# Up projections of a gated ConvFFN: from feature-major, one feature tile at a time, to token-major, four at a time

## The chip, the core and the metric

The kernel runs on one core of a Trainium2 chip. The metric is the device time in microseconds, as the median of several runs. A core has TensorE (PE, matrix products; its weight loads are listed as PEld), VectorE (DVE), ScalarE (ACT), GpSimd (POOL) and SyncE (SP), each with a queue of its own that is worked off in order; SP and POOL issue the DMAs here.

## The reference

The model is an encoder of two layers over 256 tokens with 2048 channels. The even layer has a dilated-window and a differential attention, the odd one a grouped-query and a neighbourhood attention; each layer ends in a gated ConvFFN. Only the ConvFFN and what lies next to it are changed:

```python
D_MODEL = 2048; SEQ = 256; DEPTH = 2; D_FF = 5632; CONV_W = 3

def conv_ffn(x, w_up, conv_w, conv_b, w_down):
    h = jnp.einsum("bsd,df->bsf", x, w_up)
    g, u = h[..., :D_FF], h[..., D_FF:]
    gp = jnp.pad(g, ((0, 0), (1, 1), (0, 0)))
    g = conv_w[0] * gp[:, :-2] + conv_w[1] * gp[:, 1:-1] + conv_w[2] * gp[:, 2:] + conv_b
    return jnp.einsum("bsf,fd->bsd", jax.nn.gelu(g) * u, w_down)

def reference(...):
    for layer in range(DEPTH):
        ...
        h = h + mix.astype(h.dtype)
        f = conv_ffn(rmsnorm(h, ln_ffn[layer]), ...)
        h = h + f.astype(h.dtype)
    return rmsnorm(h, ln_final)
```

All inputs are float32. The gate g and the factor u have 5632 features each, which are 44 tiles of 128. The convolution runs along the tokens.

## The kernel before

**Numbers.** Every operand of a product is split into a high part of type fp32r and the rest, also fp32r; a product is the sum high x high, low x high and high x low. `split` (L239) does it: ScalarE casts the high part (L240), VectorE subtracts it (L243). Weights come in units of 128 x 1024 values (512 KB): `wunit` (L116) loads one on SP's queue into one of RAW = 5 buffers and splits it into one of four pairs wh, wl.

**Two forms of a product.** In the feature-major form, `gemm_b` (L151), the weight block of 128 x 128 is stationary and the activations move: `b_high` (L140, matmul at L142) streams 512 columns, the 256 tokens of the high and of the low part side by side; `b_low` (L146, matmul at L148) streams the 256 tokens of the high part once more for wl. The result has features on the partitions and two halves of 256 columns, which `halves` (L230) adds: ScalarE copies one (L233), VectorE adds the other (L234) and multiplies by the row factor of the RMS norm (L236), which has to be broadcast over the partitions for it (`row_broadcast`, L337, two TensorE transposes). In the token-major form, `gemm_a` (L208), 128 tokens of the activations are stationary and 512 features of the weights move (`a_products`, L198, matmuls at L204 to L206): for each unit two blocks of 128 channels, two token halves and three products, twelve matmuls. The result has tokens on the partitions, in two PSUM banks.

**The ConvFFN** (`ffn`, L789). The 44 feature tiles are worked in two halves of 22, since the product tiles of more than 24 don't fit. For each tile one `gemm_b` gives gate and factor, VectorE convolves along the tokens (three instructions, L810, L812, L814), ScalarE applies GELU (L816), VectorE multiplies (L818) and the product is split into a tile prod. After 22 tiles the down projection runs token-major over four chunks of 512 channels (`finish_chunk(gemm_a(...))`), each of 11 units, and VectorE adds its result to the residual h (L361).

**From residual to the next product.** After the last half, the squares of each chunk are summed on ScalarE (L274). Chunks 0 to 2 are turned to feature-major by `turned_rows` (L317): VectorE transposes 32 x 32 blocks within a 128 x 1024 tile (L320), and `moved` (L278) puts the blocks in place by 16 DMAs of 32 KB, by turns from POOL's and SP's queue (L282). Then ScalarE and VectorE make the split tiles yT. Chunk 3 is turned by TensorE (`transposes`, L309, at L305). `mixer_out` (L369) does the output projection of the attention in the same way, but works chunks 0 and 1 side by side up to the last unit, so that the last attention head has time to arrive. The attention uses the pair `turned` (L286) and `moved` for its probabilities.

**The order of the work.** The program is written out flat. `later(delay, fn)` (L91) keeps a step for a later tick; `tick` (L95) is called after every second unit of a `gemm_a` and twice in a `gemm_b`, and emits what is due; `flush` (L103) emits all that is pending. When the program is built, the framework plans the order of each engine's queue from the order of emission and from durations that it assumes; buffers that are not yet free hold an instruction back. What is marked `keep_in_program_order` stays where it was emitted. On the chip each queue then runs in that fixed order, and an instruction that waits holds back those behind it.

**The end.** `finish_all` (L1010) does the last down projection, chunk by chunk, with the final norm; the last four units of chunk 3 are split ahead and worked first for one half of the tokens, then for the other.

## Time and profile before

| | us |
|---|---|
| median of 3 runs | 2456.17 (2455.28 to 2456.97) |
| profiled execution | 2455.45 |
| its span, first to last instruction | 2453.7 |
| TensorE busy | 2441.5 (100%) |
| VectorE busy | 1631.3 (66%) |
| ScalarE busy | 1261.4 (51%) |
| GpSimd busy | 165.2 (7%) |

The page of the profile lists busy times, the chain of work that ended last (followed back from the last instruction), and the costliest groups of instructions with the idle time ahead of them and what ended it. The views of the trace used here are: the chain in order of time (start, length, what), TensorE's waits (us in all, times, longest), a timeline by engine (start, length, instruction, and in brackets the idle time before it and its releaser), and tables of busy time by stretch. A mean in ns is that of one instruction from its start to its end; matmuls overlap, so the distance of their starts is shorter than that.

### The profile page before, as it was taken

To read this page: it belongs to the slowest core of one execution; us is meant where nothing else is said; L and a number is where in the kernel's file an instruction comes from. 1 tells how busy PE (TensorE), PEld (TensorE's weight loads), DVE (VectorE), ACT (ScalarE), POOL (GpSimd) and SP (SyncE) were. 2 spreads that over 40 slices of the span, in tenths; PEclk is the share of its full clock that TensorE was granted. 3 is DMA by queue.
4 is the path that set the end of the run, shared out by engine and by line. 5 is a ranking of instruction groups with operands and counts; after the bars stand their busy time and mean duration, and the time that the engine had idled before them with its cause. 6 is when DMAs were issued, how large, how long until landed. Compare 5 with 4: busy or idle time off the path is not lost.

```text
span 2453.7 us, 35020 instructions
## 1 busy us (share of the span) xinstructions
PE 2441.5 (100%) x12958; PEld 2110.6 (86%) x12958; DVE 1631.3 (66%) x2472; ACT 1261.4 (51%) x1876; POOL 165.2 (7%) x292
## 2 busy tenths in 40 slices
PE   9999999999999999999999999999999999999998
PEld 8888888888888888888888888888888888888887
DVE  6577577677677774476775567766777754676754
ACT  6455455565654543445444557545555533545443
POOL 1011012011200000000001100332000000000000
PEclk9999999999999999999999999999999999999999
DMA  8566566555655566555556655657556565555564
GB/s 309 183 201 194 171 190 207 177 183 196 208 173 199 180 198 202 182 193 185 195 193 202 218 186 157 192 170 243 180 182 197 183 208 191 180 194 185 197 197 146
DMA packets 183212, 474.00 MB, mean 193 GB/s; under 512 B 65144, under 2 KB 66936, under 8 KB 183040
## 3 DMA queue, kind: packets, MB, share of 16 engines
q1 hardware_dynamic: 173264, 460.03, 56.9%
q0 software_dynamic: 9344, 11.08, 2.5%
q8 instruction: 101, 1.65, 0.3%
q10 hardware_dynamic: 432, 0.66, 0.1%
q14 instruction: 71, 0.58, 0.1%
HBM read 458.48 MB, written 2.18 MB: 188 GB/s over the span
## 4 chain that ended last, share of the span: by engine, by line
PE 97%; DVE 1%; issue 1%; ACT 0%; DMA 0%; POOL 0%; SPq 0%; DVEq 0%; ACTq 0%
PE gm L142 38%; PE gm L148 20%; PE gm L205 12%; PE gm L204 12%; PE gm L206 12%; PE tp L305 0%; DMA room<-scc 0%; POOL room L282 0%; PE s L426 0%; PE s L428 0%; PE s L427 0%; PE s L661 0%; DVE wl L243 0%; SPq L282 0%; PE s L622 0%
## 5 line engine op out<-in xcount | busy, mean ns | idle before, releaser
L243 DVE TENSOR_TENSOR wl<-raw,wh 128x1024 fp32r<-128x1024 f32 (+1 forms) x860 | 1034.3, 1216 | 558.2 <-ACT wh L240 325.7
L240 ACT CAST wh<-raw 128x1024 fp32r<-128x1024 f32 (+1 forms) x860 | 897.2, 1047 | 704.5 <-PE gm L206 377.6
L142 PE MATMUL gm<-yT,wh 128*128 128x512 f32 x4096 | 954.6, 390 | 0.0
L142 PEld LDWEIGHTS gm<-yT,wh 128*128 128x128 f32 x4096 | 760.6, 188 | 153.9 <-DVE yT L249 1.0
L148 PEld LDWEIGHTS gm<-yT,wl 128*128 128x128 f32 x4096 | 507.6, 192 | 9.2
L148 PE MATMUL gm<-yT,wl 128*128 128x256 f32 x4096 | 511.9, 283 | 0.0
L204 PE MATMUL gm<-wh,prod 128*128 128x512 f32 x702 | 273.1, 389 | 0.0
L205 PE MATMUL gm<-wl,prod 128*128 128x512 f32 x702 | 273.1, 389 | 0.0
L206 PE MATMUL gm<-wh,prod 128*128 128x512 f32 x702 | 273.1, 389 | 0.0
L233 ACT COPY t<-gm 128x256 f32<-128x256 f32 x256 | 95.4, 373 | 283.1 <-PE gm L148 282.9
L204 PE MATMUL gm<-wh,yT 128*128 128x512 f32 x412 | 161.2, 392 | 0.0
L205 PE MATMUL gm<-wl,yT 128*128 128x512 f32 x412 | 160.8, 390 | 0.0
L206 PE MATMUL gm<-wh,yT 128*128 128x512 f32 x412 | 160.7, 390 | 0.0
L205 PEld LDWEIGHTS gm<-wl,prod 128*128 128x128 f32 x702 | 131.8, 188 | 27.4
L204 PEld LDWEIGHTS gm<-wh,prod 128*128 128x128 f32 x702 | 131.8, 188 | 27.4
L206 PEld LDWEIGHTS gm<-wh,prod 128*128 128x128 f32 x702 | 131.8, 188 | 27.1
L234 DVE TENSOR_TENSOR t<-t,gm 128x256 f32<-128x256 f32 x256 | 105.6, 413 | 1.5 <-ACT t L233 1.3
L205 PE MATMUL gm<-wl,mix 128*128 128x512 f32 x256 | 100.0, 390 | 2.1 <-DVE wl L243 2.1
L204 PE MATMUL gm<-wh,mix 128*128 128x512 f32 x256 | 100.0, 390 | 0.6 <-ACT mix L246 0.6
L206 PE MATMUL gm<-wh,mix 128*128 128x512 f32 x256 | 99.3, 389 | 0.0
L282 POOL DMA_DIRECT2D hT<-z x72 | 41.5, 584 | 780.9 <-ACT junk L274 681.0
L206 PEld LDWEIGHTS gm<-wh,yT 128*128 128x128 f32 x412 | 77.4, 188 | 16.1
(248 smaller groups left out, 1640.0 us busy)
## 6 DMA issues: line engine op xcount, KB each, us to landing
raw<-in_up SPq DMA_DIRECT2D x352, 512.0 KB, 4.3
raw<-in_down SPq DMA_DIRECT2D x176, 512.0 KB, 4.3
raw<-in_eva_qk SPq DMA_DIRECT2D x96, 512.0 KB, 4.2
raw<-in_eva_v SPq DMA_DIRECT2D x46, 512.0 KB, 4.4
raw<-in_evb_qk SPq DMA_DIRECT2D x32, 512.0 KB, 4.1
raw<-in_ev_out SPq DMA_DIRECT2D x32, 512.0 KB, 4.6
raw<-in_od_qk SPq DMA_DIRECT2D x32, 512.0 KB, 4.4
raw<-in_od_out SPq DMA_DIRECT2D x32, 512.0 KB, 4.4
```

The lines of the kernel that those rows point to most:

```text
L142: T.matmul(ps.rearrange("p a b -> p (a b)"), wh[:, k * P:(k + 1) * P], act[u * 8 + k].rearrange("p a b -> p (a b)"), start=(u == 0 and k = ...
L148: T.matmul(ps[:, 1, :], wl[:, k * P:(k + 1) * P], act[u * 8 + k][:, 0, :], start=False, stop=(last and u * 8 + k == KT - 1))
L204: T.matmul(ps[t], ah, wh[:, sl], start=(kt == 0), stop=False)
L205: T.matmul(ps[t], ah, wl[:, sl], start=False, stop=False)
L206: T.matmul(ps[t], al, wh[:, sl], start=False, stop=(kt == nk - 1))
L233: S.copy(t0, ps[:, 0, :])
L234: V.tensor_tensor(t0, t0, ps[:, 1, :], op=ALU.add)
L240: first = S.copy(dst_h, src)
L243: V.tensor_tensor(dst_l, src, dst_h.bitcast(F32), op=ALU.subtract)
L282: (nc.sync if i % 2 else G).dma_start(dst[j * 32:(j + 1) * 32, :, i * 32:(i + 1) * 32], z[i * 32:(i + 1) * 32].rearrange("p (b j c) -> p b ...
```

## The change

The up projections use `gemm_a`: a group is four feature tiles, and each of its two sides (gate, factor) is one product of 8 units with 512 features. ScalarE scales the result by the row factor on its way out of PSUM, VectorE transposes the 32 x 32 blocks, and 16 DMAs move them into a feature-major tile of 128 x 1024 (a quad). Two ticks later the four gate tiles are convolved, and GELU is applied to all four at once; two ticks after the factor's product the four are multiplied and split. The halves have 24 and 20 tiles, that is 6 and 5 groups. The down projection works its first two chunks side by side up to the last two units of each, which need the last group's tiles. The attention's q and k tiles lie in quads of the same size as the pairs of before; the differential attention's turned probabilities and the xT tiles of the start lie in other buffers. The weights of up and down are laid out in the new order of units on the host.

```diff
@@ -288,9 +288,6 @@
         V.transpose(p, p)
         moved(p, dst)
 
-    def new_turned(tag, n=4, pool=att):
-        return pool.tile([P, n, P], F32, name=nm("pf"), tag=tag, bufs=1)
-
     def y_tile(src, gain, kt, pin=False):
         y = acts.tile([P, 2, SEQ], F32R, name=nm("yT"), tag="yT", bufs=KT)
         dst = [y[:, x, :] for x in range(2)]
@@ -395,8 +392,13 @@
             return pairs[slot - slot % 2][:, slot % 2]
         return acts.tile([P, 2, SEQ], F32R, name=nm(name), tag=f"act{slot}")
 
+    def quad(slot, dtype=F32):
+        return att.tile([P, 4, SEQ], dtype, name=nm("qk"), tag=f"qk{slot}", bufs=1)
+
     def new_qk(name, slot):
-        return att.tile([P, 2, SEQ], F32R, name=nm(name), tag=f"qk{slot}", bufs=1)
+        if slot % 2 == 0:
+            pairs["qk", slot] = quad(slot, F32R)
+        return pairs["qk", slot - slot % 2][:, slot % 2 * 2:slot % 2 * 2 + 2, :]
 
     def qk_sum(ps, r, order, slot):
         t = halves(ps, r, order)
@@ -488,12 +490,12 @@
 
 
     def x_load(u):
-        t = att.tile([P, 2, SEQ], F32, name=nm("xT"), tag=f"qk{2 + u % 4}", bufs=1)
+        t = acts.tile([P, 2, SEQ], F32, name=nm("xT"), tag=f"act{u % 4}")
         nc.sync.dma_start(t.rearrange("p a b -> p (a b)"), a["xT"][u])
         return t
 
     ln = load("ln", (P, 4, KT), eng=nc.sync)
-    xt0 = att.tile([P, 2, SEQ], F32, name=nm("xT"), tag="qk2", bufs=1)
+    xt0 = acts.tile([P, 2, SEQ], F32, name=nm("xT"), tag="act0")
     nc.scalar.dma_start(xt0[:, 0, :], a["xT"][0, :, 0:SEQ])
     zeros = tmp.tile([P, SEQ], F32R, name="zeros", tag="rx")
     V.memset(zeros.bitcast(F32), 0.0)
@@ -737,7 +739,7 @@
             V.tensor_scalar(w[:, t, 1, :], w[:, t, 1, :], den[:, t, 1:2], None, op0=ALU.mult)
             V.scalar_tensor_tensor(w[:, t, 0, :], w[:, t, 0, :], den[:, t, 0:1], w[:, t, 1, :],
                                    op0=ALU.mult, op1=ALU.add)
-        pf = new_turned(f"qk{4 + hd % 2}")
+        pf = b_room[:, hd % 2 * 4:hd % 2 * 4 + 4]
         turned(sc[0][:, 0, :], pf)
         later(3, lambda: b_transposes(hd, pf, vt), 1)
 
@@ -774,6 +776,7 @@
             split_scaled(natural(y[:, 0, :]), natural(y[:, 1, :]), parity_rev(ps[:, f, :]), sub_gain[:, f:f + 1])
             mix[8 + 2 * hd + f] = y
 
+    b_room = quad(4).rearrange("p a (b c) -> p (a b) c", c=P)
     for pair in range(2):
         vt = v_tiles(gemm_a(a["evb_v"][pair], yT, KT), rstd_par, range(20 - 4 * pair, 24 - 4 * pair))
         for hd in (2 * pair, 2 * pair + 1):
@@ -786,46 +789,76 @@
     yT = mixer_out(a["ev_out"], mix, ln[:, 2, :])
 
 
+    def up_group(layer, j, yT, rstd, prod):
+
+        sides = {}
+        for x in range(2):
+            ps = gemm_a(a["up"][layer, j, x], yT, KT, hooks={6: flush} if not (j or x) else {})
+            if not (j or x):
+                rstd.append(row_factor())
+            z = new_sc().rearrange("p t (f k) -> p (t f) k", k=P)
+            for t in range(2):
+                S.activation(z.rearrange("p (f t) k -> p t f k", t=2)[:, t], ps[t].rearrange("p (f k) -> p f k", k=P),
+                             AF.Copy, scale=rstd[0][:, t:t + 1])
+            sides[x] = quad(2 * x)
+            turned(z.rearrange("p b k -> p (b k)"), sides[x].rearrange("p f (t k) -> p (f t) k", k=P))
+            if not x:
+                later(2, lambda: convolved(layer, j, sides))
+        later(2, lambda: multiplied(j, sides, prod))
+
+    def convolved(layer, j, sides):
+
+        g4, c4 = sides[0], quad(4)
+        sides[2] = c4
+        for i in range(4):
+            f = 4 * j + i
+            g, c = g4[:, i, :], c4[:, i, :]
+            V.tensor_scalar(c, g, convw[:, layer, 1, f:f + 1], convb[:, layer, f:f + 1], op0=ALU.mult, op1=ALU.add)
+            V.scalar_tensor_tensor(c[:, 1:SEQ], g[:, 0:SEQ - 1], convw[:, layer, 0, f:f + 1],
+                                   c[:, 1:SEQ], op0=ALU.mult, op1=ALU.add)
+            V.scalar_tensor_tensor(c[:, 0:SEQ - 1], g[:, 1:SEQ], convw[:, layer, 2, f:f + 1],
+                                   c[:, 0:SEQ - 1], op0=ALU.mult, op1=ALU.add)
+        S.activation(c4, c4, AF.Gelu_apprx_tanh)
+
+    def multiplied(j, sides, prod):
+
+        u4, c4 = sides[1], sides[2]
+        V.tensor_tensor(c4, c4, u4, op=ALU.mult)
+        for i in range(4):
+            y = new_act("prod", (4 * j + i) % NACT)
+            split(y[:, 0, :], y[:, 1, :], c4[:, i, :])
+            prod.append(y)
+
+    def first_two(src, act, nk, done):
+
+        pss = [[tps("gm", 4), tps("gm", 4)] for _ in range(2)]
+        for c in range(2):
+            for u in range(nk // 2 - 2):
+                a_unit(pss[c], src[c], u, act, nk)
+                if u % 2 == 1:
+                    tick()
+        flush()
+        for c in range(2):
+            for u in range(nk // 2 - 2, nk // 2):
+                a_unit(pss[c], src[c], u, act, nk)
+            done(pss[c], c)
+
     def ffn(layer, yT, gain, last=False):
-        R = None
-        res = None
-        for half in range(2):
+        rstd, res = [], None
+        for g0, g1 in ((0, 6), (6, 11)):
             prod = []
-            for i in range(HALF_F):
-                f = half * HALF_F + i
-                srcs = [a["up"][layer, f, x] for x in range(2)]
-                if f == 0:
-                    rstd = []
-
-                    def first_units():
-                        flush()
-                        rstd.append(row_factor(late=True))
-
-                    pg, pu = gemm_b(srcs, yT, first_units)
-                    R = row_broadcast(rstd[0], pin=True)
-                else:
-                    pg, pu = gemm_b(srcs, yT)
-                g = halves(pg, R)
-                c = tmp.tile([P, SEQ], F32, name=nm("cv"), tag="cv")
-                V.tensor_scalar(c, g, convw[:, layer, 1, f:f + 1], convb[:, layer, f:f + 1],
-                                op0=ALU.mult, op1=ALU.add)
-                V.scalar_tensor_tensor(c[:, 1:SEQ], g[:, 0:SEQ - 1], convw[:, layer, 0, f:f + 1],
-                                       c[:, 1:SEQ], op0=ALU.mult, op1=ALU.add)
-                V.scalar_tensor_tensor(c[:, 0:SEQ - 1], g[:, 1:SEQ], convw[:, layer, 2, f:f + 1],
-                                       c[:, 0:SEQ - 1], op0=ALU.mult, op1=ALU.add)
-                S.activation(c, c, AF.Gelu_apprx_tanh)
-                u = halves(pu, R)
-                V.tensor_tensor(c, c, u, op=ALU.mult)
-                y = new_act("prod", f % NACT)
-                split(y[:, 0, :], y[:, 1, :], c)
-                prod.append(y)
-            if half:
+            for j in range(g0, g1):
+                up_group(layer, j, yT, rstd, prod)
+            nk = 4 * (g1 - g0)
+            src = [a["down"][layer, c, 2 * g0:2 * g1] for c in range(4)]
+            if g0:
                 res = []
                 if last:
-                    finish_all(a["down"][layer, half], prod, y)
+                    finish_all(src, prod, nk)
                     return
-            for c in range(4):
-                finish_chunk(gemm_a(a["down"][layer, half, c], prod, HALF_F), c, gain, res)
+            first_two(src, prod, nk, lambda ps, c: finish_chunk(ps, c, gain, res, 1 + c))
+            for c in range(2, 4):
+                finish_chunk(gemm_a(src[c], prod, nk), c, gain, res)
         return res
 
     yT = ffn(0, yT, ln[:, 1, :])
@@ -1007,18 +1040,22 @@
         S.activation(g[:, sls[1]], g[:, sls[1]], AF.Copy, scale=r)
         nc.scalar.dma_start(rows(1536, 2048), g)
 
-    def finish_all(src, act, y):
-
-        S.activation(warm, y[:, 0, 0:1].bitcast(F32), AF.Square)
-        S.activation(warm, warm, AF.Sqrt)
-        nu = HALF_F // 2
-        for c in range(3):
-            finish_chunk(gemm_a(src[c], act, HALF_F), c, None, [])
-            later(1, lambda c=c: gained(c))
+    def finish_all(src, act, nk):
+
+        def done(ps, c):
+            if not c:
+                S.activation(warm, act[-1][:, 0, 0:1].bitcast(F32), AF.Square)
+                S.activation(warm, warm, AF.Sqrt)
+            finish_chunk(ps, c, None, [])
+            later(1, lambda: gained(c))
+
+        nu = nk // 2
+        first_two(src, act, nk, done)
+        done(gemm_a(src[2], act, nk), 2)
         later(1, first_chunks)
         ps = [tps("gm", 4), tps("gm", 4)]
         for u in range(nu - AHEAD):
-            a_unit(ps, src[3], u, act, HALF_F)
+            a_unit(ps, src[3], u, act, nk)
             if u == 1:
                 tick()
         kept = [(u, wunit(src[3][u])) for u in range(nu - AHEAD, nu)]
@@ -1027,7 +1064,7 @@
             ssq = [tmp.tile([P, 1], F32, name=nm("ssl"), tag="ss1") for _ in range(2)]
             v = tmp.tile([P, 1], F32, name=nm("var"), tag="var1")
             for u, w in kept[:-1] if t else kept:
-                a_products(ps, w, u, act, HALF_F, [(t, 0), (t, 1)])
+                a_products(ps, w, u, act, nk, [(t, 0), (t, 1)])
             if t:
                 halved(ps[t], apart, *kept[-1], act)
             finish_half(t, 0, ps[t][:, sls[0]], ssq, v)
@@ -1132,10 +1169,8 @@
     r["od_v"] = _chunks_a(wd[:, 2048:])
     r["od_out"] = _chunks_a(i["od_w_out"][0])
 
-    up = i["ffn_w_up"].reshape(2, 2, 8, P, 2, FT, P)
-    r["up"] = up.transpose(0, 5, 4, 1, 3, 2, 6).reshape(2, FT, 2, 2, P, UN)
-    down = i["ffn_w_down"].reshape(2, 2, HALF_F // 2, 2, P, 4, 512)
-    r["down"] = down.transpose(0, 1, 5, 2, 4, 3, 6).reshape(2, 2, 4, HALF_F // 2, P, UN)
+    r["up"] = np.stack([np.stack([_chunks_a(w[:, :DFF]), _chunks_a(w[:, DFF:])], axis=1) for w in i["ffn_w_up"]])
+    r["down"] = np.stack([_chunks_a(w) for w in i["ffn_w_down"]])
     return {k: np.ascontiguousarray(v) for k, v in r.items()}
 
 
```

## The prediction

> **What bounds the kernel now.** I read the page first: which engine is busy, and what the chain of waits consists of.
>
> ```profile
> span 2453.7 us, 35020 instructions
> PE 2441.5 (100%) x12958; PEld 2110.6 (86%) x12958; DVE 1631.3 (66%) x2472; ACT 1261.4 (51%) x1876; POOL 165.2 (7%) x292
> PE 97%; DVE 1%; issue 1%; ACT 0%; DMA 0%; POOL 0%; SPq 0%; DVEq 0%; ACTq 0%
> PE gm L142 38%; PE gm L148 20%; PE gm L205 12%; PE gm L204 12%; PE gm L206 12%; PE tp L305 0%; DMA room<-scc 0%; POOL room L282 0%; PE s L426 0%; PE s L428 0%; PE s L427 0%; PE s L661 0%; DVE wl L243 0%; SPq L282 0%; PE s L622 0%
> ```
>
> TensorE is busy in 2441.5 of 2453.7 us, and the chain is 97% TensorE. Nothing else can give time back: a change helps only if TensorE gets the same products done in less time, and hurts only if it makes TensorE wait. Next, the waits of TensorE alone, and the busy times of the stages that the change touches: the feature-major up projections (20 of 22 features), the down projection of the first half, the up and the down projection of the second half.
>
> ```profile
> PE gm L205 <- DVE wl L243: 2.1, 2, 1.1
> PE s L505 <- DVE warm L501: 1.2, 1, 1.2
> PE gm L204 <- ACT mix L246: 0.6, 1, 0.6
> PE tp L305 <- DVE ob L765: 0.6, 1, 0.6
> PE tp L305 <- DVE ry L868: 0.4, 1, 0.4
> core 0: us, PE busy (x) PEld busy (x) DVE busy (x) ACT busy (x) POOL busy (x), PEclk, DMA share, GB/s
> 691.85:914.12 222.27, 222.27 (x1282) 196.86 (x1281) 158.54 (x261) 111.43 (x160) 0.00 (x0) 1.00 0.58 190
> 914.12:1033.83 119.71, 119.71 (x529) 99.11 (x529) 61.44 (x60) 46.45 (x46) 0.00 (x0) 1.00 0.62 201
> 1278.30:1397.84 119.54, 119.54 (x529) 98.93 (x529) 69.96 (x75) 55.19 (x70) 20.28 (x33) 1.00 0.71 218
> ```
>
> TensorE waits 4.9 us in the whole run, and in these stages not at all. Its clock is 1.00 in all of them. So the question is what one weight block costs TensorE in either form; the chain in order of time says it.
>
> ```profile
> 691.85 7.28 PE gm L142 x32
> ...
> 903.00 7.28 PE gm L142 x32
> 910.28 3.83 PE gm L148 x32
> 914.12 0.23 PE gm L204
> ...
> 1033.83 7.25 PE gm L142 x32
> ```
>
> A feature (gate and factor, 32 weight blocks of 128x128) recurs every (903.00 - 691.85) / 19 = 11.113 us: 32 matmuls of 512 columns in 7.28 us (227.5 ns each) and 32 of 256 columns in 3.83 us (119.7 ns each). The token-major down projection does 4 chunks x 11 units x 12 = 528 matmuls of 512 columns in 1033.83 - 914.12 = 119.71 us: 226.7 ns each. Half of 226.7 is 113.4, so a 256-column matmul pays 6.3 ns more than its columns: two rows through one line (512 columns 226.7, 256 columns 119.7) give 0.418 ns a column and 12.7 ns a matmul whatever its width.
>
> **The change part by part.**
>
> *Up projections token-major.* Columns streamed are the same: before, a block takes 512 + 256 columns; after, four blocks take six matmuls of 512, which is 768 a block. But a block now has 1.5 matmuls in place of 2. Before: four features 4 x 11.113 = 44.45 us. After: one group of four features has 2 sides x 8 units x 12 = 192 matmuls, 192 x 0.2267 = 43.53 us. The gain is 0.92 us a group, and 22 groups (11 in each of two layers) make **20.3 us**. That the down projection's rate holds with the tile yT as the stationary side is seen where the odd layer's first token-major product starts:
>
> ```profile
> 1397.84 0.39 PE L204 MATMUL gm<-wh,yT 128*128 128x512 f32 x1
> ...
> 1403.05 0.39 PE L206 MATMUL gm<-wh,yT 128*128 128x512 f32 x1
> ```
>
> 23 steps in 5.21 us are 226.5 ns each. The Trainium skill bears on this term ("TensorE: Matmul & The Clock Gate", section "Back-to-back issue gap"): warm, it has a gap of N/2.4 + 2.5 ns, 262 cycles for 256 columns and 518 for 512. By its figures a block would go from 780 cycles to 777, an estimate of 1.25 ns, and the 2816 blocks would gain 3.5 us. The rows above disagree: the fixed part is 12.7 ns here, not 2.5, and the sum goes by the rows.
>
> *The row factor.* After a token-major product the factor is a number per partition, applied by ScalarE. The broadcast through TensorE (line L343) goes:
>
> ```profile
> by line: PE gm L142 36.9%; PE gm L206 15.9%; PE gm L205 15.8%; PE gm L204 15.5%; PE gm L148 14.4%; PE tp L305 1.5%; PE tp L343 0.4%
> ```
>
> 0.4% of this 60 us window is 0.24 us, once a layer: **0.5 us**. The eight transposes of L305 (last chunk of the residual) stay, moved by the hook ahead of unit 6; they have TensorE products before and after them in either place.
>
> *Gate and factor turned.* Each of the 44 sides adds two ScalarE copies with scale out of PSUM, one VectorE transpose of 128x1024, and 16 DMAs, eight on SP's queue and eight on POOL's. The same transfer (a 128x1024 tile, 16 DMAs) is in the trace nine times (72 DMAs of SP, eight each), after residual chunks; here are two of them by engine, and one smaller transfer whose reader waited longest, with TensorE's waits in the 40 us around it (1640 to 1680).
>
> ```profile
> hT<-z SPq DMA_DIRECT2D x72, 32.0 KB, 2.3
> 1308.27 1.06 ACT L240 CAST wh<-raw 128x1024 fp32r<-128x1024 f32 x1 [1.67 <-PE gm L206]
> 1309.10 1.25 DVE L320 STREAM_TRANSPOSE z<-h 128x1024 f32<-128x1024 f32 x1
> 1310.37 5.17 SPq L282 DMA_DIRECT2D hT<-z  x8
> 1315.66 3.44 SPq L125 DMA_DIRECT2D raw<-in_down  x4
> 1315.98 0.58 POOL L282 DMA_DIRECT2D hT<-z  x1 [1.04 <-DMA hT<-z]
> 1316.43 1.05 ACT L240 CAST wh<-raw 128x1024 fp32r<-128x1024 f32 x1 [1.67 <-DMA hT<-z]
> 1320.18 1.71 ACT L246 ACTIVATE yT<-hT,ln 128x256 fp32r<-128x256 f32 x4 [2.69 <-DMA hT<-z]
> 1339.02 1.25 DVE L320 STREAM_TRANSPOSE z<-h 128x1024 f32<-128x1024 f32 x1
> 1348.01 1.71 ACT L246 ACTIVATE yT<-hT,ln 128x256 fp32r<-128x256 f32 x4 [0.60 <-issue]
> 1646.33 0.62 ACT L240 CAST pt<-room 128x512 fp32r<-128x512 f32 x1 [9.03 <-DMA room<-scc]
> PE gm L205 <- DVE wl L243: 1.1, 1, 1.1
> ```
>
> From the end of the transpose to the first reader pass 9.83 us in the one (1310.35 to 1320.18) and 7.74 in the other (1340.27 to 1348.01). On SP's queue the weights behind the transfer are held 5.2 us, and before it for as long as the transpose is late. What hides that: weights are loaded five buffers and split four units ahead, and a unit feeds TensorE for 12 x 0.2267 = 2.72 us. The trace bears it out: the window 1278.30 to 1397.84 holds three such transfers and TensorE is busy in all of it. Without that cover a transfer would cost its 5.2 us of issue, 44 times. The DMA engines have room: that window has a share of 0.71 where the same stage without transfers has 0.62, so 0.09 x 119.5 = 10.8 us of all engines for three transfers and some loads, 3.6 us each at most; two in 43.5 us add 0.17 and bring the up stage to some 0.79.
>
> Cost of the 44 transfers to TensorE, from both sides: below, 0, as after all nine of the same form; above, 1.1 us each, the longest wait of TensorE for a weight split in the list of waits, 48 us. I take the lower end, because the nine are the same transfer beside the same product.
>
> *Convolution and product.* Work on VectorE, by groups:
>
> ```profile
> L243 DVE TENSOR_TENSOR wl<-raw,wh 128x1024 fp32r<-128x1024 f32 x852 | 1028.9, 1221 | 556.6 <-ACT wh L240 324.1 <-PE gm L148 231.8
> L234 DVE TENSOR_TENSOR t<-t,gm 128x256 f32<-128x256 f32 x256 | 105.6, 413 | 1.5 <-ACT t L233 1.3
> L236 DVE TENSOR_TENSOR t<-t,R 128x256 f32<-128x256 f32 x216 | 90.5, 420 | 0.0
> L814 DVE SCALAR_TENSOR_TENSOR cv<-t,convw,cv 128x255 f32<-128x255 f32 x88 | 41.8, 475 | 0.1
> L812 DVE SCALAR_TENSOR_TENSOR cv<-t,convw,cv 128x255 f32<-128x255 f32 x88 | 41.8, 475 | 0.0
> L810 DVE TENSOR_SCALAR cv<-t,convw,convb 128x256 f32<-128x256 f32 x88 | 35.7, 406 | 0.0
> 1465.13 0.69 ACT L845 ACTIVATE rx<-gm,rstd 128x512 f32<-128x512 f32 x1 [0.26 <-PE gm L206]
> ```
>
> VectorE had 158.54 / 5 = 31.7 us in four features. A group loses eight pairs of L234 and L236, 8 x 0.833 = 6.7 us, and gains two transposes, 2.5 us: 27.5 of 43.5 us, 63% for 71%. No engine comes near TensorE. What changes is the grain: the twelve convolution instructions of a group now come in one run of 4 x (0.406 + 0.475 + 0.475) = 5.4 us, and the first of them waits for a transfer; queued behind it on VectorE are weight splits, for which TensorE waits. That wait is new, and it is the step on which I am least sure; it is costed as a rival.
>
> *First two chunks side by side.* The last product tiles are late by a transfer; the down projection now covers that with 2 x 10 units (first half) or 2 x 8 (second) of older tiles, 16 x 2.72 = 43.5 us at least against a delay of some 20. Matmul count is the same: 0. Halves of 24 and 20 tiles move work between halves and take none away: 0. xT in other buffers, quads in place of pairs, and the weight layout (512 KB a unit as before) have no TensorE work and the same number of DMAs: 0.
>
> *Sum.* 20.3 + 0.5 = 20.8 us. The profiled execution took 2455.45 us (its span 2453.7 and 1.75 around it), which gives 2434.7; the median of the runs shown is 0.72 above that execution, so 2435.4, and I say **2435.5 us**.
>
> **The rivals.** A measurement here tells 0.2%, 4.9 us, from no change.
>
> *A: the splits behind the convolution come late, now and then.* Let TensorE end a gate side at 0. The second scaled copy ends at 0.26 + 0.69 = 1.0, the transpose at 2.25, the transfer lands at 2.25 + 7.74 = 10.0, the convolution ends at 15.4, and a split placed behind it at 16.6. The queue orders are fixed when the program is built; the reader at 1320.18 stands behind the fourth split after the chunk's end (1308.27 to 1316.43 in steps of 2.72), which is that for unit 6 of the next product, since units 0 to 2 were split before. If the convolution stands before that split, unit 6 is due at 6 x 2.72 = 16.3 and is 0.3 us late: 22 x 0.3 = 6.6, and the time is 2442. For it: the reader at 1320.18 waited 2.69 us, so the order was planned for an earlier landing. Against it: behind that split, the next is due at 19.0, and nothing is late.
>
> *B, slower: the same, each time with the late landing.* With 9.83 us the transfer lands at 12.1, the convolution ends at 17.5, the split of unit 6 at 18.7, 2.4 us late: 22 x 2.4 = 53 us, and 2455.45 - 20.8 + 53 + 0.7 = 2488. It decides from 0.92 us a group on, the whole gain. For it: the pt reader blocked ScalarE's queue for 9.03 us, and TensorE's 1.1 us wait for a split falls in the same 40 us. Against it: 9.83 was the worst of the nine, with another DMA in its way.
>
> *C, no change: the 6.3 ns come back.* If the token-major rate in the up stage were 347.2 / 1.5 = 231.5 ns a matmul, nothing would be gained but the 0.5 us: 2455.7. For it: the last bits of the working are small, 7.1 ns in a block of 347. Against it: two stages with different stationary tiles show 226.5 to 226.7 ns. The skill's rule as worked out above would end here too, at 2456.2 - 3.5 = 2452.7; the same rows speak against it.
>
> That the change doesn't do what it says I can exclude as far as the text goes: the 5632 instructions of L142 and L148 in the up stage are replaced in the program.
>
> **How the numbers follow.** Forecast (2432 to 2439): 0.62. A (2439 to 2451): 0.18. C, or a mixture of A and B that eats the gain (2451 to 2461): 0.08. B (above 2461): 0.09. A gain larger than the sum (below 2432): 0.03. The range takes the forecast and A, 2431 to 2451, which leaves out less than 2 in 10. Faster: 0.62 + 0.18 + 0.03 = 0.83; same 0.08; slower 0.09.
>
> **What would show it.** In the profile after: lines L142 and L148 keep 1280 matmuls each, and the up stage has 192 matmuls of 512 columns in 43.5 us a group (right), or more (C). A group for TensorE waiting on wl (L243) with a count near 22 or 44 would be A or B, with its mean as the price. VectorE idle before the first convolution instruction, released by a DMA, tells how much too early it stands; up to 3 us is harmless by the working above. VectorE should fall and POOL gain 352 DMA instructions. TensorE gaps where down begins would show the last tiles late, and weights landing late on SP's queue would show the transfers in the way. Wrong would be a TensorE busy time that doesn't fall by about 20 us, or idle time of more than a few us beside it.

## The result and the profile after

| | before | after |
|---|---|---|
| median, us | 2455.73 (2455.21 to 2456.97) | 2432.3 (2432.15 to 2432.95) |
| profiled span, us | 2453.7 | 2430.4 |
| TensorE matmuls | 12958 | 11546 |

After to before is 0.9904, with a 95% interval of 0.9887 to 0.9922: faster by 23.4 us. The forecast was 2435.5, a gain of 20.8, so the time lies inside the range of 2431 to 2451 and 3.2 us below the forecast. The page of the kernel after, with the rows that answer to those of before (busy times, the chain that ended last by engine and by line, the two feature-major lines and one token-major line):

```profile
span 2430.4 us, 33216 instructions
PE 2419.1 (100%) x11546; PEld 2036.5 (84%) x11546; DVE 1562.1 (64%) x2092; ACT 1248.0 (51%) x1722; POOL 367.0 (15%) x644
PE 97%; DVE 1%; DMA 1%; ACT 0%; issue 0%; SPq 0%; DVEq 0%; ACTq 0%
L142 PE MATMUL gm<-yT,wh 128*128 128x512 f32 x1280 | 298.4, 390 | 0.0
L148 PE MATMUL gm<-yT,wl 128*128 128x256 f32 x1280 | 160.2, 283 | 0.0
L204 PE MATMUL gm<-wh,yT 128*128 128x512 f32 x1820 | 709.2, 390 | 0.0
```

TensorE still sets the end, and its busy time fell by 22.4 us. L142 and L148 keep the 1280 matmuls of the attentions. POOL has 352 instructions more (292 to 644), as the steps said. VectorE has 69.2 us less, where the steps gave some 92 (31.7 to 27.5 us in each of 22 groups); it bounds nothing here.

Where the time came from is read by stage: the ConvFFN of layer 0, the odd layer's attention, the ConvFFN of layer 1 to the end. The bounds are the first matmul of each stage in the chain in order of time (1397.84 is from the timeline, by the chain it is 1398.00, which would move 0.2 us of the gain from the attention to the first ConvFFN); the table is that of busy time by stretch, before and then after (columns: length, then busy time and instructions of PE, weight loads, DVE, ACT and POOL, the granted clock, DMA share, GB/s).

```profile
668.21:1397.84 729.63, 729.63 (x3884) 632.03 (x3883) 477.16 (x702) 350.88 (x474) 20.28 (x33) 1.00 0.60 193
1397.84:1716.48 318.64, 316.16 (x1632) 270.24 (x1631) 225.49 (x379) 186.76 (x351) 64.14 (x110) 1.00 0.61 189
1716.48:2453.70 737.22, 729.85 (x3889) 632.30 (x3887) 474.65 (x710) 350.78 (x477) 0.00 (x0) 1.00 0.57 187
```

```profile
668.55:1387.54 718.99, 718.99 (x3178) 595.63 (x3177) 443.03 (x512) 344.57 (x397) 121.61 (x209) 1.00 0.71 212
1387.54:1703.76 316.22, 315.51 (x1631) 270.24 (x1631) 225.12 (x379) 186.09 (x351) 63.55 (x110) 1.00 0.63 191
1703.76:2430.40 726.64, 719.05 (x3182) 595.52 (x3181) 439.86 (x520) 344.19 (x400) 101.14 (x176) 1.00 0.68 205
```

The two ConvFFNs give 10.64 and 10.58 us, 21.2 together, where the sum had 20.8; each has some 706 matmuls fewer (704 from the form, 2 from the broadcast of the row factor). The odd attention, which the sum had at nothing, gives 2.4. (The start of the kernel takes 0.3 us more, so that the three make 23.3 us of span.) TensorE is busy from end to end of the ConvFFN in layer 0 although 22 transfers now run in it. The list of TensorE's waits after the change has no group with a count near 22 or 44, the sign of rivals A and B:

```profile
PE s L507 <- DVE warm L503: 1.2, 1, 1.2
PE gm L204 <- ACT mix L246: 0.6, 1, 0.6
PE tp L302 <- DVE ob L767: 0.6, 1, 0.6
PE gm L195 <- ACT wh L240: 0.5, 1, 0.5
PE tp L302 <- DVE ry L901: 0.4, 1, 0.4
PE gm L205 <- DVE wl L243: 0.3, 1, 0.3
```

### The profile page after: what moved, and what is told of

It reads as the page before. It is cut to its first block, busy times and chain, and to the rows that moved or that the text cites. A ratio compares the mean times of both kernels' runs of the same rounds, so it can differ in the third digit from the quotient of the medians.

```text
span 2430.4 us, 33216 instructions
## 1 busy us (share of the span) xinstructions
PE 2419.1 (100%) x11546; PEld 2036.5 (84%) x11546; DVE 1562.1 (64%) x2092; ACT 1248.0 (51%) x1722; POOL 367.0 (15%) x644
## 4 chain that ended last, share of the span: by engine, by line
PE 97%; DVE 1%; DMA 1%; ACT 0%; issue 0%; SPq 0%; DVEq 0%; ACTq 0%
PE gm L204 26%; PE gm L205 26%; PE gm L206 26%; PE gm L142 12%; PE gm L148 6%; PE tp L302 0%; PE s L428 0%; PE s L430 0%; PE s L429 0%; DVE wl L243 0%; PE s L663 0%; DMA raw<-in_od_out 0%; PE s L624 0%; SPq L282 0%; DMA raw<-in_eva_v 0%
## 5 line engine op out<-in xcount | busy, mean ns | idle before, releaser
L204 PE MATMUL gm<-wh,yT 128*128 128x512 f32 x1820 | 709.2, 390 | 0.0
L205 PE MATMUL gm<-wl,yT 128*128 128x512 f32 x1820 | 708.6, 389 | 0.0
L206 PE MATMUL gm<-wh,yT 128*128 128x512 f32 x1820 | 708.5, 389 | 0.0
L205 PEld LDWEIGHTS gm<-wl,yT 128*128 128x128 f32 x1820 | 341.8, 188 | 70.8 <-DVE wl L243 0.7
L204 PEld LDWEIGHTS gm<-wh,yT 128*128 128x128 f32 x1820 | 341.6, 188 | 71.0 <-ACT junk L274 0.4
L206 PEld LDWEIGHTS gm<-wh,yT 128*128 128x128 f32 x1820 | 341.7, 188 | 70.8
L282 POOL DMA_DIRECT2D qk<-sc x384 | 219.7, 580 | 1135.0 <-DVE sc L288 1037.9
L142 PE MATMUL gm<-yT,wh 128*128 128x512 f32 x1280 | 298.4, 390 | 0.0
L142 PEld LDWEIGHTS gm<-yT,wh 128*128 128x128 f32 x1280 | 237.8, 188 | 48.0
L206 PE MATMUL gm<-wh,prod 128*128 128x512 f32 x702 | 273.1, 389 | 0.0
L148 PE MATMUL gm<-yT,wl 128*128 128x256 f32 x1280 | 160.2, 283 | 0.0
L148 PEld LDWEIGHTS gm<-yT,wl 128*128 128x128 f32 x1280 | 158.1, 192 | 2.3
L206 PEld LDWEIGHTS gm<-wh,prod 128*128 128x128 f32 x702 | 131.8, 188 | 27.5
L206 PE MATMUL gm<-wh,mix 128*128 128x512 f32 x256 | 99.3, 389 | 0.0
```

The source lines that it names most:

```text
L142: T.matmul(ps.rearrange("p a b -> p (a b)"), wh[:, k * P:(k + 1) * P], act[u * 8 + k].rearrange("p a b -> p (a b)"), start=(u == 0 and k = ...
L148: T.matmul(ps[:, 1, :], wl[:, k * P:(k + 1) * P], act[u * 8 + k][:, 0, :], start=False, stop=(last and u * 8 + k == KT - 1))
L204: T.matmul(ps[t], ah, wh[:, sl], start=(kt == 0), stop=False)
L205: T.matmul(ps[t], ah, wl[:, sl], start=False, stop=False)
L206: T.matmul(ps[t], al, wh[:, sl], start=False, stop=(kt == nk - 1))
L282: (nc.sync if i % 2 else G).dma_start(dst[j * 32:(j + 1) * 32, :, i * 32:(i + 1) * 32], z[i * 32:(i + 1) * 32].rearrange("p (b j c) -> p b ...
```

## The experiments

Three questions were open. Is it the number of matmuls that gave the 20 us, and does a matmul cost the same 12.7 ns at every width? Are the transfers free because of the depth of the prefetch, and how far does it reach? Does the place of the convolution in VectorE's queue decide rivals A and B? Every kernel does the whole computation; the runs that move a tile twice add copies that nobody reads. Each is compared with the kernel before on the same chip (2455.05 to 2455.46 us) and with the 2432.3 of the kernel after.

**Buffers alone.** The kernel before, with only the attention's quads, its turned probabilities and the xT tiles in the buffers of after:

```diff
+    def quad(slot, dtype=F32):
+        return att.tile([P, 4, SEQ], dtype, name=nm("qk"), tag=f"qk{slot}", bufs=1)
...
-        t = att.tile([P, 2, SEQ], F32, name=nm("xT"), tag=f"qk{2 + u % 4}", bufs=1)
+        t = acts.tile([P, 2, SEQ], F32, name=nm("xT"), tag=f"act{u % 4}")
...
-        pf = new_turned(f"qk{4 + hd % 2}")
+        pf = b_room[:, hd % 2 * 4:hd % 2 * 4 + 4]
```

> The kernel before with only the edits outside the ConvFFN: q and k tiles in quads, the probabilities of the differential attention in one of them, xT in other buffers. Of the 23.3 us by which the span fell, 2.4 lie in the odd layer's attention (318.6 to 316.2 us), which the prediction had at nothing; TensorE's wait there for a weight split fell from 2.1 to 0.3 us. Theory 1, the buffers did it: the odd attention takes 316 us here too, and the time is 2.4 below before, 2453.3. Theory 2, the buffers have no part in it and the other plan of the queue orders did it: within 0.5 us of before, the wait stays at about 2 us.

Measured: 2455.69 us (2454.94 to 2459.03), ratio 1.0003 (0.9994 to 1.0013). The buffers change nothing; TensorE's wait for a weight split in the odd layer, which is gone in the kernel after, is still there (2.1 us in two waits). The gain in the odd attention isn't theirs.

**The number of matmuls, put back.** In the up products of the kernel after, the matmul of the weights' low part is issued as two, of 256 and 256 columns, or of 128 and 384. Columns and data stay; there are 2 sides x 8 units x 4 x 22 groups = 1408 matmuls more.

```diff
-            T.matmul(ps[t], ah, wl[:, sl], start=False, stop=False)
+            for c0, c1 in ((0, cut[0]), (cut[0], 512)) if cut[0] else ((0, 512),):
+                T.matmul(ps[t][:, c0:c1], ah, wl[:, k * 512 + c0:k * 512 + c1], start=False, stop=False)
...
+            cut[0] = 256
             ps = gemm_a(a["up"][layer, j, x], yT, KT, hooks={6: flush} if not (j or x) else {})
+            cut[0] = None
```

> The changed kernel, with each product of the low weights in the up projections done as two matmuls of 256 columns in place of one of 512: 1408 matmuls more, the same columns. Theory, a fixed cost of 12.7 ns a matmul: 2 x 119.7 in place of 226.7 ns, so 1408 x 12.7 = 17.9 us more, 2450. Rival, the old form was slow for another reason than the number of matmuls (its halves in one PSUM bank, its order): no change, 2432.

> As the run with two times 256 columns, but 128 and 384. Theory, a straight line of 12.7 ns a matmul and 0.418 ns a column: the same 17.9 us more, 2450. Rival, the 256-column matmul is not bound by its columns at all but by its weight load, a floor of some 120 ns: 120 + 173 in place of 226.7 ns, 1408 x 66 = 93 us more, 2525.

Measured: 2455.51 us with 256 and 256 (ratio 1.0000, 0.9991 to 1.0010), 23.2 above the kernel after; 2533.32 with 128 and 384 (1.0315, 1.0299 to 1.0330), 101.0 above. Per added matmul this is 23.2 / 1408 = 16.5 ns and 101.0 / 1408 = 71.7 ns. The expectation of 17.9 us for both was missed, by 5 us with the even cut and by far with the uneven one. The chain in order of time shows where the time lies; L208 is the cut matmul (two in one row), L209 and L206 are the whole ones. First 256 and 256:

```profile
719.83 0.23 PE gm L206
720.06 0.23 PE gm L208 x2
720.29 0.23 PE gm L209
```

Then 128 and 384:

```profile
719.89 0.23 PE gm L206
720.12 0.29 PE gm L208 x2
720.40 0.23 PE gm L209
```

At this resolution only the uneven pair grows, to 0.29. The first question has its answer in the even cut: the same columns in the old number of matmuls (each with a weight load of its own) bring the old time back. That the whole agrees to 0.2 us with the 2455.30 of before is partly luck. By the chain the two ConvFFNs take 2.1 us more than in the kernel before (730.71 and 738.37 us against 729.79 and 737.22), and the odd attention between them 2.1 less (316.42 against 318.48). An added matmul costs 16.5 ns, one taken away by the change had given (21.2 - 0.5) / 1408 = 14.7. The straight line of the prediction falls in the uneven cut: by it both cuts cost 12.7 ns a matmul, some 18 us in all.

**A cut between them.** Either a matmul has a least cost up to some width, or an uneven pair costs more as such. A cut at 192 and 320 tells them apart:

```diff
+            cut[0] = 192
             ps = gemm_a(a["up"][layer, j, x], yT, KT, hooks={6: flush} if not (j or x) else {})
+            cut[0] = None
```

> As the runs with 256 + 256 and 128 + 384 columns, but 192 + 320. The pair of 128 + 384 took 0.297 us in place of 0.2267, that of 256 + 256 0.242. Theory, a floor of some 120 ns for a matmul of 256 columns and fewer, and above it 0.417 ns a column and 13 ns: 120 + 147 = 267 ns, 1408 x 40 = 57 us more, 2489. Rival, a cost that falls on any uneven cut: about the 101 us of 128 + 384, 2533. Rival, a straight line down to 192 columns: as 256 + 256, 2455.

Measured: 2496.40 us (ratio 1.0164, 1.0149 to 1.0179), 64.1 above after, 45.5 ns per added matmul, where a floor of 120 ns gave 40 and a cost of uneven cuts as such 72. The starts of the records between 700 and 900 us say which instruction the time goes to (mean distance to the next start, ns):

| cut | from the first part | from the second part | the pair | from each whole one |
|---|---|---|---|---|
| none | | | 226.7 | 226.3 to 227.0 |
| 256 + 256 | 114.6 | 115.8 | 230.4 | 232.9 to 233.3 |
| 192 + 320 | 90.3 | 168.3 | 258.6 | 233.8 to 234.2 |
| 128 + 384 | 59.2 | 227.5 | 286.7 | 230.8 to 233.6 |

The narrow part lets the next matmul start after 59 or 90 ns; it is the wide part behind it that is long: 384 columns take as much as 512. The weight loads tell why. Here are one pair of 128 + 384 on TensorE, with the second part in a row of its own, the two loads that follow, and the next whole matmul:

```profile
719.96 0.45 PE L208 MATMUL gm<-wl,yT 128*128 128x128 f32 x2
720.02 0.39 PE L208 MATMUL gm<-wl,yT 128*128 128x384 f32 x1
719.96 0.19 PEld L208 LDWEIGHTS gm<-wl,yT 128*128 128x128 f32 x1
720.07 0.19 PEld L209 LDWEIGHTS gm<-wh,yT 128*128 128x128 f32 x1
720.24 0.39 PE L209 MATMUL gm<-wh,yT 128*128 128x512 f32 x1
```

The wide part's load begins some 3 ns after the narrow part has started. The next load begins 108 ns later in both uneven cuts, though the narrow part takes 59 ns in one and 90 in the other, and of the 12,954 loads of the run with 128 + 384 all but ten begin 107 ns or more after the one before. If the wide part can only begin 108 ns after its load, and then takes what the line gives for its columns (146.5 and 173.2 ns), the pairs come to an estimate of 3 + 108 + 146.5 = 258 and 3 + 108 + 173.2 = 284 ns, against 258.6 and 286.7 measured. By this reading two matmuls with loads of their own follow one another by 110 ns or so at the least, however narrow the first is; an extra cost of uneven pairs as such would have been as large at 192 as at 128. At 256 columns the runs can't tell the two apart, since the columns alone take 256 x 0.418 = 107 ns. The 4 to 8 ns more on each whole neighbour of a pair are unexplained. The kernel before has 128-column matmuls too, TensorE's transposes, and they show the same distance (0.87 / 8 us = 109 ns each, where the line gives 66):

```profile
670.93 0.87 PE tp L305 x8
```

**One layer at a time.** The new ConvFFN in layer 0 only, with the old one in layer 1; and the reverse.

```diff
-    yT = ffn(0, yT, ln[:, 1, :])
+    yT = ffn_b(0, yT, ln[:, 1, :])
```

(This is the reverse; `ffn_b` is the ConvFFN of before, with its weights in the old layout beside the new.)

> The new ConvFFN in layer 0 alone, the old one in layer 1, the other edits as in the changed kernel. Theory, the gain is so many blocks at so much each: half of 21.2, 10.6 us below before, 2444.5, and the odd layer's attention, which follows, tells whether its 2.4 us come from what runs ahead of it (316 us there, 2442) or not (318.6 us, 2444.5).

> The new ConvFFN in layer 1 alone, the old one in layer 0. The other half: 10.6 us below before, 2444.5; 2442 with 316 us in the odd layer's attention if its 2.4 us come from what follows it (the up projection's weights on SP's queue).

Measured: layer 0 alone 2442.43 us (0.9948, 0.9933 to 0.9963), 12.9 below the 2455.32 of before; layer 1 alone 2444.01 (0.9953, 0.9936 to 0.9970), 11.3 below. The sum is 24.2 where both together gave 23.4: the gains add up, within what a comparison tells. The odd attention between the two takes 317.4 us in the first run and 318.2 in the second, between the 318.64 of before and the 316.22 of after.

**The transfers twice.** After each side, the same 16 DMAs once more, into a tile that nobody reads:

```diff
             turned(z.rearrange("p b k -> p (b k)"), sides[x].rearrange("p f (t k) -> p (f t) k", k=P))
+            twin = att.tile([P, 8, P], F32, name=nm("twin"), tag="pt", bufs=2)
+            moved(z.rearrange("p b k -> p (b k)"), twin)
```

> The changed kernel, with the 16 DMAs of each of the 44 sides issued a second time into a tile that nothing reads: double the issue on SP's and POOL's queues (5.2 us more a side on SP) and double the block traffic (share of the DMA engines from 0.73 to some 0.9). Theory, the transfers lie behind the weights loaded and split ahead: within 2 us of the changed kernel, 2432 to 2434. Rival, the transfers already use up that cover and a second set shows: up to 44 x 5.2 = 229 us more, and anything over 5 us would speak for it.

Measured: 2518.46 us (ratio 1.0260, 1.0234 to 1.0287), 86 above the kernel after. The theory that a second transfer is hidden like the first fell. Two causes were possible, the traffic and the time for which the weights' loads stand behind the transfers on SP's queue. The next two runs take one half of the second set each: all of it issued by POOL, or only the eight DMAs of SP and none of POOL's.

```diff
-    def moved(z, dst):
+    def moved(z, dst, odd=None):
...
-                (nc.sync if i % 2 else G).dma_start(
+                (odd or nc.sync if i % 2 else G).dma_start(
...
+            moved(z.rearrange("p b k -> p (b k)"), twin, G)
```

> As the run with the second set of 16 DMAs a side, which took 86 us more than the changed kernel, but all of the second set issued from POOL's queue. There SP held the weights for some 13 us at each side (wait for the transpose, 5.2 us for the first set, 5.2 to 6 for the second) and ScalarE's casts waited for raw weights. Theory, it is SP's hold that is too long for the weights loaded ahead: here SP is held as in the changed kernel, so within 5 us of it, 2432 to 2437, though the DMA engines carry the same blocks. Rival, the block traffic itself or the landing of the weights behind it: most of the 86 us stay, 2500 or above.

Measured: 2507.00 us (ratio 1.0208, 1.0193 to 1.0224). This run doesn't separate the causes: POOL's DMAs follow one another so late that they still read the source tile when ScalarE wants to write the next side into it, and ScalarE's queue, with the weights' casts, stands behind. A row of ScalarE's timeline:

```profile
742.03 1.27 ACT L801 ACTIVATE sc<-gm,rstd 128x512 f32<-128x512 f32 x2 [3.09 <-DMA twin<-sc]
```

```diff
-    def moved(z, dst):
+    def moved(z, dst, rows=range(4)):
...
-        for i in range(4):
+        for i in rows:
...
+            moved(z.rearrange("p b k -> p (b k)"), twin, (1, 3))
```

> As the run with the second set of 16 DMAs a side (86 us more than the changed kernel), but only the eight of SP's queue: half the added block traffic, the same hold of SP, POOL as in the changed kernel. The run with the whole second set on POOL's queue took 75 us more, but there ScalarE waited for the source tile that POOL's late DMAs still read, so it didn't separate the two. Theory, SP's hold of some 13 us a side makes the weights late: most of the 86 us stay, 2500 to 2520. Rival, the block traffic on the DMA engines: half of it or less, 2475 or below.

Measured: 2512.25 us (ratio 1.0236, 1.0219 to 1.0253), 80 above after, with half of the added traffic. The kernel after first: a 200 us stretch of the first half's up stage, ScalarE's longest wait of a cast for a DMA in the ConvFFN, then SP's queue.

```profile
700.00:900.00 200.00, 200.00 (x884) 165.68 (x883) 133.00 (x164) 101.26 (x118) 41.39 (x72) 1.00 0.74 220
```

```profile
ACT wh L240 <- DMA qk<-sc: 31.6, 19, 1.7
```

```profile
742.12 14.41 SPq L125 DMA_DIRECT2D raw<-in_up  x8
758.53 5.54 SPq L282 DMA_DIRECT2D qk<-sc  x8
764.19 14.10 SPq L125 DMA_DIRECT2D raw<-in_up  x8
```

And with SP's eight DMAs twice: the same stretch, the two longest waits of TensorE with one of ScalarE, and SP's queue.

```profile
700.00:900.00 200.00, 190.30 (x810) 153.91 (x809) 121.91 (x154) 90.91 (x105) 36.89 (x64) 0.97 0.69 208
```

```profile
PE gm L204 <- ACT wh L240: 33.2, 18, 2.8
PE gm L205 <- DVE wl L243: 12.6, 26, 1.1
ACT wh L240 <- DMA raw<-in_up: 143.8, 126, 5.0
```

```profile
737.07 5.25 SPq L282 DMA_DIRECT2D qk<-sc  x8
742.37 6.08 SPq L282 DMA_DIRECT2D twin<-sc  x8
748.49 10.71 SPq L125 DMA_DIRECT2D raw<-in_up  x9
```

The DMA engines are less busy than in the kernel after (0.69 against 0.74), an up unit takes 4.8 us from issue to landing in the median where it took 4.4, and yet TensorE waits: the traffic has a small part at most. SP issues transfers for 11.4 us in one stretch (737.07 to 748.45) in place of 5.5; the weights behind them come late (ScalarE waits 143.8 us for up weights in 126 casts, where the longest such group of the kernel after, put down to a transfer landing at the time, has 31.6 us in 19), and through the casts TensorE comes to a stop. In front of the casts on which TensorE waits there is one thing more. In 18 of the 22 groups GELU stands behind four casts of its side on ScalarE's queue, where in the kernel after it stands behind six, and there ScalarE waits 7 to 8 us for the convolution. The cast behind it then still waits 0.9 to 3.4 us for its weights in each of the 18, so the weights come last, but the plan of ScalarE's queue is not the one of the kernel after.

Of the 78.1 us of span over the kernel after, 44.7 are idle time of TensorE. They aren't spread over the 44 sides: 41.4 us of the two waits shown come behind a gate's transfers, in those 18 groups (2.3 us each), and 4.4 behind a factor's, where SP is held about as long. The other 33.4 us are TensorE busy time (2452.5 against 2419.1). The clock records of the trace have TensorE busy for 39.6 us at half clock, which makes 19.8 of them. Another 7 are an estimate: a matmul ahead of a wait counts to its end (0.39 us), any other to the start of the next (0.23), and there are 44 such waits. The rest is open.

**The place of the convolution.** The weight splits on VectorE were kept behind the convolution, from unit 4 of the factor's product on, or from unit 6 on, which is the order that rivals A and B supposed:

```diff
+        rest = V.tensor_tensor(dst_l, src, dst_h.bitcast(F32), op=ALU.subtract)
+        if kept:
+            tc.keep_in_program_order(rest)
...
+            hooks = {6: flush} if not (j or x) else {6: lambda: kept.append(1)} if x else {}
+            ps = gemm_a(a["up"][layer, j, x], yT, KT, hooks=hooks)
+            kept.clear()
...
-                later(2, lambda: convolved(layer, j, sides))
+                later(3, lambda: convolved(layer, j, sides))
```

(With unit 4 the hook is at 4 and the tick stays 2.)

> The changed kernel, with the convolution held ahead of the weight split for unit 4 of the factor's product on VectorE's queue (in the changed kernel it stands behind that for unit 6). Theory, the place in the queue decides: the transfer lands 10.0 to 11.8 us after the gate's product, the twelve instructions take 4.5, the split 1.2, so it is done at 15.7 to 17.5 where unit 4 is due at 11.1: 4.6 to 6.4 us late in each of 22 groups, 100 to 140 us more, 2532 to 2572. Rival, VectorE's order has no weight because splits are far enough ahead: 2432.

> The same, with the convolution held ahead of the split for unit 6: this is the order of rival A and B of the prediction. Theory: done at 15.7 to 17.5 where unit 6 is due at 16.6, so 0 to 0.9 us late a group, 0 to 20 us more, 2432 to 2452, with 2439 the likeliest. Rival, order without weight: 2432.

Measured: from unit 4 on 2566.56 us (ratio 1.0452, 1.0436 to 1.0468), 134 above after; from unit 6 on 2435.12 (0.9917, 0.9902 to 0.9932), 2.8 above, which is less than a comparison tells from nothing. VectorE then waits ahead of the convolution in every group (36.1 us in 22 waits), but TensorE's waits for weight splits are only 1.8 us, in two waits, where after has 0.3; the run's span is 2.0 above that of after. With the splits held from unit 4 on, VectorE idles until the transfer has landed and then finds the splits waiting:

```profile
692.59 1.18 DVE L245 TENSOR_TENSOR wl<-raw,wh 128x1024 fp32r<-128x1024 f32 x1
702.13 0.73 DVE L822 TENSOR_SCALAR qk<-qk,convw,convb 128x256 f32<-128x256 f32 x2 [8.36 <-DMA raw<-in_up]
...
706.58 4.62 DVE L245 TENSOR_TENSOR wl<-raw,wh 128x1024 fp32r<-128x1024 f32 x4
```

```profile
PE gm L205 <- DVE wl L245: 86.9, 23, 6.2
```

In the kernel after, the same stretch has the convolution behind three more splits, those of units 4 to 6:

```profile
691.98 1.25 DVE L288 STREAM_TRANSPOSE sc<-sc 128x1024 f32<-128x1024 f32 x1 [1.13 <-ACT sc L801]
...
700.50 1.23 DVE L243 TENSOR_TENSOR wl<-raw,wh 128x1024 fp32r<-128x1024 f32 x1 [1.50 <-ACT wh L240]
703.09 0.74 DVE L816 TENSOR_SCALAR qk<-qk,convw,convb 128x256 f32<-128x256 f32 x2 [1.36 <-DMA raw<-in_up]
...
707.54 3.50 DVE L243 TENSOR_TENSOR wl<-raw,wh 128x1024 fp32r<-128x1024 f32 x3
```

Order decides, not the landing: the same transfer costs nothing in one place, at most some 3 us one split earlier and 134 three splits earlier.

**Chunk by chunk.** The down projection's first two chunks one after the other, as before, not side by side:

```diff
-            first_two(src, prod, nk, lambda ps, c: finish_chunk(ps, c, gain, res, 1 + c))
-            for c in range(2, 4):
+            for c in range(4):
...
-        first_two(src, act, nk, done)
-        done(gemm_a(src[2], act, nk), 2)
+        for c in range(3):
+            done(gemm_a(src[c], act, nk), c)
```

> The changed kernel, with the down projection chunk by chunk as before, in place of the first two side by side. Theory, the last product tiles are some 16 us late and ten or eight units of older tiles (27 or 21.8 us) are cover enough: within 1 us of the changed kernel, no wait of TensorE for prod. Rival, the side-by-side order is what hides them: TensorE waits for prod once in each of the four halves, 5 us or more each, 2452 or above.

Measured: 2432.26 us (2431.39 to 2432.48; ratio 0.9904, 0.9889 to 0.9918), the time of the kernel after. TensorE waits for no product tile in that run. The new order of the chunks has no part in the result.

## Why the prediction was right, and where it wasn't

**The up projections.** Right in sign, place and size: 20.8 us was said for the two ConvFFNs, 21.2 came. The number of matmuls, each with its weight load, is shown to be the cause by the even cut, which puts 1408 of them back and takes the whole gain of the ConvFFNs away (23.2 us for 21.2), and the two layers alone add up. No run tells a matmul from its load in this. The Trainium skill ("TensorE: Matmul & The Clock Gate", section "Back-to-back issue gap"), by whose figures the gain would have been an estimated 3.5 us, isn't borne out by this kernel; nor is rival C.

**The line behind it.** The step "12.7 ns a matmul whatever its width" was drawn through two points, 512 and 256 columns, and doesn't hold below them: by it the cut into 128 and 384 adds 12.7 ns, and it added 71.7. The gain came out right since it rests on the two points alone: 17.9 of the 20.3 us are 1408 x 12.7 ns, the rest the 0.8 ns by which each of the 2816 512-column matmuls was longer in the old form (227.5 against 226.7). What holds below 256 columns is the distance of the weight loads, 107 ns or more. The same page of the Trainium skill (section "LDWEIGHTS (loading the stationary operand)") gives P/1.2 ns for P columns, by which 128 columns take an estimated 107 ns; the 108 ns between the loads of the uneven cuts agree. That the load sets the distance is read from the starts of the records and from two pairs that come out of it; no run had narrower weights, so it wasn't tried.

**The transfers.** Said at 0, and 0 it was: TensorE is busy in 718.99 of 718.99 us of layer 0's ConvFFN. The cover was named rightly (the depth of the prefetch, against the hold on SP's queue), and its reach wasn't worked out. Two transfers in a row on SP's queue, 11.4 us, already cost 2.3 us of idle time at a gate's side in 18 groups, and three quarters as much again in TensorE's busy time, some 20 us of it through the lower clock. The second hold is 5.2 to 6.1 us, so the slack left in the kernel after is estimated at 3 to 4 us at a gate's side and some 5 at a factor's, as far as a run with another plan on ScalarE's queue tells. The forecast of the run with two transfers failed on just this.

**Rivals A and B.** The late landing of B did occur: in the first group the gate's product began at 668.55 and ended 96 x 0.2267 + 0.87 us later (the 0.87 are the transposes of the residual), at 691.2, and the convolution began at 703.09, 11.9 later, where B had 12.1. But it stands behind the split of unit 6 (the one at 700.50), as the argument against A had it; the split of unit 7 is then done at 707.54 + 1.2 = 708.7, and is due at 691.2 + 7 x 2.72 = 710.2. The prediction left the order open, and the order is what decided. Its price for A, 6.6 us for the wrong order, was at most some 3 when it was tried; B's 53 didn't come even so, because the landing is late in few groups. The convolution's first line shows this in the kernel after: 3.6 us in two waits, 1.4 of them in the first group. By the trace the last block lands 6.6 to 8.1 us after the transpose in 20 of the 22 groups, and 9.4 and 10.3 in the two others; the prediction had 7.74 for A and 9.83 for B.

```profile
L816 DVE TENSOR_SCALAR qk<-qk,convw,convb 128x256 f32<-128x256 f32 x88 | 32.1, 407 | 3.6 <-DMA raw<-in_up 3.6
```

(The view names a weight load as releaser. The instruction reads the quad alone, so what it waits for is the transfer; the two land at about the same time.)

**Side by side, and the buffers.** Both were said at 0 and tried alone, and neither moved the time by more than 0.4 us.

**The step that was off.** "No TensorE work and the same number of DMAs: 0" left out the odd attention, which no step touched and which gave the missing 2.4 us. Its TensorE idle time fell from 318.64 - 316.16 = 2.5 us to 0.7: the wait for a weight split (2.1 us, in the prediction's list of waits) is nearly gone; the other 0.6 us are busy time. The stage takes 316.2 to 317.1 us in the kernel after and in those with cut matmuls (256 and 128) or the chunks one by one, 318.6 and 319.4 in the kernel before and with the buffers alone. So it isn't the buffers' doing. Nor is it fixed by the attention's own code, which is that of the kernel after in the runs with the convolution from unit 4 on and with the second set on POOL's queue: there the stage takes 319.7 and 324.0 us (3.4 and 6.8 of them at half clock). Between the two runs of one layer, the stage is the shorter where the ConvFFN ahead of it is the new one (317.4) but both have a part (318.2 in the other). The orders of all queues are planned over the whole program, so another program ahead or behind can give this stage another order; that this is the cause was not shown, and it stays open.

## What to carry to other kernels

When TensorE is the bound at full clock, count its matmuls and weight loads beside its columns: here an operand cut from 512 to 256 moving columns cost 6 to 8 ns a half, and one cut into 128 and 384 cost 71.7 ns, because, by the trace, the loads begin no less than 107 ns apart. A short row of the profile that nobody needs for the sum, here the eight transposes, can test a line drawn through two points. Work that is put behind a deep prefetch is free only up to that depth, and a profile in which it is free doesn't show how near the edge is: doubling it does, here from 0 to 80 us. Where a queue holds both feeders of the bound engine and a reader of a late transfer, the place of the reader in that queue is worth more than the lateness.

## What was not expected of the hardware

A pause of TensorE costs more than its length. With the convolution ahead of unit 4, TensorE waited 86.9 us for splits and the kernel lost 134. The table of busy time in steps of 2 us around one such wait shows the rest (the clock granted is the number before the DMA share):

```profile
702.00:704.00 2.00, 0.00 (x0) 0.00 (x0) 1.87 (x6) 1.91 (x2) 0.00 (x0) 1.00 0.00 0
704.00:706.00 2.00, 0.00 (x0) 0.00 (x0) 2.00 (x7) 0.00 (x0) 0.00 (x0) 0.58 0.00 0
706.00:708.00 2.00, 0.14 (x1) 0.15 (x1) 2.00 (x4) 1.06 (x1) 0.00 (x0) 0.50 0.00 0
708.00:710.00 2.00, 2.00 (x5) 1.62 (x6) 2.00 (x3) 0.00 (x0) 0.00 (x0) 0.50 0.60 152
710.00:712.00 2.00, 2.00 (x7) 1.54 (x7) 1.20 (x2) 0.02 (x1) 0.00 (x0) 0.71 0.95 356
```

In this wait the last matmul ends at 702.0 us, the clock drops to a half at 704.3, the next matmul starts at 707.9, and full clock is back at 711.1, after 3.3 us of work. In that time a 512-column matmul starts 0.43 us after the one before (708.45, 708.88, 709.30 in the timeline) in place of 0.23. In the clock records of the run, but for one at its end, the stretches at half clock last 3.4 us, or two or three times that; TensorE is busy in 95.0 us of them, and half of this, 47.5, is nearly all of the 50.4 us that TensorE's busy time grew over the kernel after (2469.5 against 2419.1). Its idle time grew by 86.5 us. A pause needn't be that long: in the run with SP's second set, with waits of at most 2.8 us, there are twelve such stretches of 3.4 us in the course of the work.

The distance of at least 107 ns between two weight loads of 128 columns is the other thing. The kernel before did show it, in its transposes, but the two rows from which the prediction drew its line lie above it.
